# Transposes of x in one pass, the convolution accumulated in PSUM, and later modulation sums, in a hybrid Conformer and mLSTM block

## The chip, the cores and the metric

The kernel runs on one core of a Trainium2 chip. The core's engines work side by side, each in the order of its own queue: TensorE (PE, with its weight loads as PEld), VectorE (DVE), ScalarE (ACT), GpSimd (POOL), and SyncE (SP), which issues most DMA transfers. SBUF holds tiles of 128 partitions. PSUM holds eight banks of 128 x 512 fp32 numbers; TensorE writes its results there, VectorE and ScalarE read and write it. The metric is the device time of one execution in microseconds (us): 1196.62 is the median of three runs before the change (1196.0 to 1198.24).

## The reference

One layer of a backbone, all in fp32: 1024 latent tokens x of width 1024 and 256 context tokens. It computes, in order:

- Modulation: `silu(c) @ w_ada + b_ada` gives six vectors of 1024 (shift, scale and gate of the two sub-layers). The same is done for the context with `c_ctx`, of which only the first two are used here.
- `h = rms_norm(x, g0) * (1 + scale) + shift`, and the same for the context.
- One projection `h @ w_in` gives a, gl (512 each), q, k, v, o (512 each) and 16 gate columns.
- Conformer group: `u = a * sigmoid(gl)`; a depthwise convolution of width 31 along grid rows of 64 tokens; LayerNorm; silu.
- mLSTM group: four heads, two directions, chunked recurrences that begin from the context's final state; a norm per head; times `sigmoid(o)`.
- The two groups side by side through `w_out`, a norm, gate and residual; then a gated feed-forward of width 2816 with its own norm, modulation and residual.

Each output of the convolution is a sum over 31 taps:

```
y[t, c] = conv_b[c] + sum over j of conv_w[j, c] * u[t + j - 15, c]    # only within the row of 64 tokens
```

## The kernel before

Channels lie on partitions and tokens along the free dimension (xT, hT, u and accf are 128 x 1024 per block of 128 channels). Every large product is made in pieces of fp32r: operands are split into a high and a low part (`split`, `mod_apply`), and three matmuls of 512 columns (high by high, high by low, low by high) stand for one (`mm_block`, lines 150 to 154). The high part is made on ACT, the low part by a two-input subtraction on DVE or POOL (lines 134, 265 and 382).

Start (lines 397 to 452, all engines in the order written): x arrives in eight tiles of 128 tokens. For each, ACT makes the sum of squares (`x_sq`), DVE and POOL the inverse root (`rsqrt_pow`, lines 140 and 141), DVE scales the identity by it (`x_rs`, line 198), and TensorE multiplies the tile by that diagonal (`x_tr`, line 204), so that the tile comes out transposed and normalised in one fp32 product. `x_evac` copies it to xT. In between stand the load and split of the first weights and the first modulation sums (`mod_sum`, line 228: one DVE instruction over 128 x 1024 for each channel block and vector).

GLU of the first two channel blocks (j = 0, 1): for each of eight blocks k of the contraction, `mod_k` sums and scales, `mod_apply` makes h in two halves of tokens, and `glu0` issues 24 matmuls. From line 453 on a scheduler sets the order of all engines but SP; within an engine it takes what is ready by its own costs, with priorities. `glu_evac` (lines 273, 274) makes u, `conv(j)` (lines 276 to 287) the convolution: ACT writes the middle tap and the bias into accf in SBUF, and 30 DVE instructions at line 286 each add one tap in place. They have the lowest priority (`prio(100000)`), so they fill what DVE has left over while TensorE goes on with j = 2 and 3, then the v projections with the gates (`vpass`, lines 556 to 558), and the heads: the projections k, q, o with `mlstm_head` woven in. All transposes and products of a head go through `pl` or `pg` and have line 508. `conv_norm` needs all four convolutions. In PSUM two pools hold four banks each, `mm` for projections and `tp` for transposes and the heads' products. `ada_step(n)` puts the next n of 32 later modulation sums (each with its 512 KB load into one of three `raw` tiles) into the program; `proj` asks for two with each of its twelve blocks of weights.

## Time and profile before

The table is of one profiled execution, whose own time was 1197.89 us, with a span of 1195.8 us from its first instruction to its last; 2.1 us lie around the span.

| engine | busy us | share of the span | instructions |
|---|---|---|---|
| PE | 1143.2 | 96% | 5463 |
| PEld | 939.5 | 79% | 5463 |
| DVE | 932.0 | 78% | 1702 |
| ACT | 523.7 | 44% | 952 |
| POOL | 121.3 | 10% | 106 |

Shares of the whole span hide the stages. Busy time of PE is an upper figure, since its matmuls overlap and their ends are modelled. What counts for a change in one stage is what that stage's PE waits for, and which engine is full there.

### The profile page before, as it was taken

What the parts mean: (1) busy time and instruction counts of PE and PEld (TensorE: products, weight loads), DVE (VectorE), ACT (ScalarE), POOL (GpSimd) and SP (SyncE); (2) the same over time, 40 slices, a digit from 0 to 9 for tenths busy, and PEclk for the clock granted to TensorE, in tenths of its full rate; (3) what the DMA queues carried; (4) which work ended last, traced back from release to release, by engine and by line L of the source; (5) the groups of instructions that cost most, each with busy time, mean ns of one, the idle gap of its engine ahead of it and who ended that gap; (6) DMA issues with size and microseconds to landing.
All of it is one profiled execution on the core that took longest, in us unless ns stands there. A gap on an engine that the chain in (4) does not pass through costs nothing.

```text
span 1195.8 us, 14940 instructions
## 1 busy us (share of the span) xinstructions
PE 1143.2 (96%) x5463; PEld 939.5 (79%) x5463; DVE 932.0 (78%) x1702; ACT 523.7 (44%) x952; POOL 121.3 (10%) x106
## 2 busy tenths in 40 slices
PE   6899898999898999999999999999999999999997
PEld 5788787877687777887787888878888878888885
DVE  4899999999779996568966676676668685995585
ACT  6432222242485454357545344343434355454461
POOL 2634120111302210010000000000000000000000
PEclk9899899999999999999999999999999999999999
DMA  8963110442225412442324231323132159633251
GB/s 305 329 207 121 52 37 1 142 147 65 88 89 176 140 56 89 150 167 89 104 73 132 88 122 55 132 89 132 45 132 93 75 192 391 227 112 117 80 220 71
DMA packets 51823, 153.42 MB, mean 128 GB/s; under 512 B 5589, under 2 KB 5925, under 8 KB 49958
## 3 DMA queue, kind: packets, MB, share of 16 engines
q1 hardware_dynamic: 40662, 132.28, 32.0%
q10 hardware_dynamic: 11088, 20.19, 4.5%
q8 instruction: 43, 0.70, 0.2%
q14 instruction: 30, 0.25, 0.1%
HBM read 123.83 MB, written 28.61 MB: 127 GB/s over the span
## 4 chain that ended last, share of the span: by engine, by line
PE 61%; DVE 6%; ACT 1%; issue 1%; POOL 0%; DVEq 0%; POOLq 0%; ACTq 0%
PE mm L1141 8%; PE mm L1143 8%; PE mm L1142 8%; PE c L1369 3%; PE c L1371 3%; PE c L1370 3%; PE tp L1143 3%; PE tp L1142 3%; PE tp L1141 3%; PE a L1369 3%; PE a L1371 3%; PE a L1370 2%; PE mm L951 2%; PE mm L953 2%; PE mm L952 2%; PE tp L508 2%
## 5 line engine op out<-in xcount | busy, mean ns | idle before, releaser
L286 DVE SCALAR_TENSOR_TENSOR s<-t,sml,s 128x864 f32<-128x864 f32 (+14 forms) x120 | 150.5, 1295 | 0.1
L150 PE MATMUL mm<-s,w 128*128 128x512 f32 (+1 forms) x320 | 126.6, 399 | 0.0
L151 PE MATMUL mm<-s,w 128*128 128x512 f32 (+1 forms) x320 | 124.7, 393 | 0.1
L133 ACT ACTIVATE w<-raw 128x1024 fp32r<-128x1024 f32 x94 | 97.0, 1054 | 20.6 <-DMA raw<-in_w_out_dram 5.3
L1141 PE MATMUL mm<-s,w 128*128 128x512 f32 x264 | 104.9, 397 | 0.7 <-ACT h L1214 0.7
L1142 PE MATMUL mm<-s,w 128*128 128x512 f32 x264 | 104.2, 395 | 0.0
L1143 PE MATMUL mm<-s,w 128*128 128x512 f32 x264 | 104.0, 395 | 0.0
L134 DVE TENSOR_TENSOR w<-raw,w 128x1024 fp32r<-128x1024 f32 x77 | 92.3, 1222 | 1.5 <-PE mm L952 0.8
L154 PE MATMUL mm<-s,w 128*128 128x512 f32 (+1 forms) x320 | 93.2, 400 | 0.0
L141 POOL TENSOR_TENSOR r<-yw,mhalf 128x1 f32<-128x1 f32 x16 | 9.7, 608 | 690.7 <-DVE yw L140 690.7
L1141 PE MATMUL mm<-x,w 128*128 128x512 f32 x176 | 70.5, 401 | 0.7 <-ACT h L1205 0.5
L151 PEld LDWEIGHTS mm<-s,w 128*128 128x128 f32 x320 | 60.9, 190 | 11.6 <-POOL s L265 0.7
L1141 PE MATMUL tp<-s,w 128*128 128x512 f32 x176 | 69.5, 395 | 0.0
L150 PEld LDWEIGHTS mm<-s,w 128*128 128x128 f32 x320 | 61.0, 190 | 10.9
L1142 PE MATMUL tp<-s,w 128*128 128x512 f32 x176 | 69.5, 395 | 0.0
L1143 PE MATMUL tp<-s,w 128*128 128x512 f32 x176 | 69.4, 394 | 0.0
L1142 PE MATMUL mm<-x,w 128*128 128x512 f32 x176 | 69.3, 394 | 0.0
L1143 PE MATMUL mm<-x,w 128*128 128x512 f32 x176 | 69.3, 394 | 0.0
L1197 DVE TENSOR_TENSOR h<-mm,h 128x512 f32<-128x512 f32 x22 | 15.2, 692 | 66.3 <-PE mm L1143 66.3
L1271 ACT ACTIVATE s<-x 128x512 fp32r<-128x512 f32 x62 | 38.4, 628 | 64.1 <-PE a L1371 25.0
L1256 DVE TENSOR_TENSOR s<-x,s 128x512 fp32r<-128x512 f32 x62 | 42.8, 695 | 29.0 <-ACT s L1271 29.0
L154 PEld LDWEIGHTS mm<-s,w 128*128 128x128 f32 x320 | 57.0, 189 | 10.2
(311 smaller groups left out, 2916.6 us busy)
## 6 DMA issues: line engine op xcount, KB each, us to landing
raw<-in_w_up_dram SPq DMA_DIRECT2D x44, 512.0 KB, 4.5
zv<-s ACTq DMA_DIRECT2D x77, 256.0 KB, 3.4
raw<-in_w_ada_dram SPq DMA_DIRECT2D x32, 512.0 KB, 4.2
t<-in_w_ada_dram SPq DMA_DIRECT2D x28, 512.0 KB, 5.8
x<-zv SPq DMA_DIRECT2D x14, 1024.0 KB, 5.0
raw<-in_wblk_dram SPq DMA_DIRECT2D x20, 512.0 KB, 4.8
d<-in_w_down_dram SPq DMA_DIRECT2D x28, 256.0 KB, 6.8
x<-zv SPq DMA_DIRECT2D x7, 768.0 KB, 4.2
```

The costliest lines, as they stand in the source:

```text
L133: act.activation(out=hi, in_=raw, func=AF.Copy)
L134: (eng or pool).tensor_tensor(out=lo, in0=raw, in1=hi.bitcast(F32), op=ALU.subtract)
L150: pe.matmul(o, w[0][:, k], hi[:, k], start=(k == 0), stop=False)
L151: pe.matmul(o, w[0][:, k], lo[:, k], start=False, stop=False)
L154: pe.matmul(o, w[1][:, k], hi[:, k], start=False, stop=(k == KT - 1))
L286: dve.scalar_tensor_tensor(out=dst, in0=uv[:, :, lo + o:hi + o], scalar=conv_w[:, j, t:t + 1], in1=dst, op0=ALU.mult, op1=ALU.add)
L1141: pe.matmul(ps, w[0][:, s], b[0][:, k], start=(start and k == 0), stop=False, skip_group_check=True)
L1142: pe.matmul(ps, w[0][:, s], b[1][:, k], start=False, stop=False, skip_group_check=True)
L1143: pe.matmul(ps, w[1][:, s], b[0][:, k], start=False, stop=(k == 3), skip_group_check=True)
L1369: pe.matmul(ps, o[:, 0, s], o[:, 2], start=start, stop=False, skip_group_check=True)
L1370: pe.matmul(ps, o[:, 0, s], o[:, 3], start=False, stop=False, skip_group_check=True)
L1371: pe.matmul(ps, o[:, 1, s], o[:, 2], start=False, stop=stop, skip_group_check=True)
```

## The change

Five things are changed together.

- Each x tile is scaled on DVE as a whole (`x_rs` over 128 x 1024) and then transposed by TensorE against the plain identity (`pe.transpose`), in place of the product with a scaled identity. Tiles 4 to 7 are transposed by channel block (`x_trk`), in two steps of 16 transposes, each followed by its own copies.
- The start is written in another order, and the part in which all engines keep the written order now reaches to the end of the GLU of blocks 0 and 1. The row of c goes through silu before it is spread over the partitions.
- `conv(j)` accumulates in PSUM: DVE writes the middle tap and bias into a pair of banks (pool `cv`), 29 taps are added there in place, and the tap of offset 1 writes the sum to accf in SBUF; the last column of each row is copied. All four convolutions use the same pair of banks.
- For that pair, `tp` has two banks in place of four. Before the convolution the pair's halves serve as tp tiles; while it runs, one of a head's tiles comes from `mm` (`HP`); from `conv_norm` on, a pool `tp2` has the pair.
- `proj` asks for no later modulation sums with the first five blocks of weights, and for four with each of the last seven.

```diff
-    tp = wide.enter_context(tc.tile_pool(name="tp", bufs=4, space=bass.MemoryType.PSUM))
+    tp = wide.enter_context(tc.tile_pool(name="tp", bufs=2, space=bass.MemoryType.PSUM))
+    cvs = wide.enter_context(ExitStack())
+    cv = cvs.enter_context(tc.tile_pool(name="cv", bufs=1, space=bass.MemoryType.PSUM))
...
+    def CV():
+        return cv.tile([P, 2, 512], F32, tag="cv", name="cv")
...
+    def HP():
+        return MM() if conv_live == [True] else TP()
...
     def x_rs(t):
         rsqrt_pow(rst[:, t:t + 1], ss[:, t:t + 1], 1, f"x{t % 2}", 1.0 / D)
-        dgx[t] = H2(P)
-        dve.tensor_scalar(out=dgx[t], in0=ident, scalar1=rst[:, t:t + 1], scalar2=None, op0=ALU.mult)
+        dve.tensor_scalar(out=xt[t], in0=xt[t], scalar1=rst[:, t:t + 1], scalar2=None, op0=ALU.mult)
...
-                pe.matmul(ps[q][:, kk * 256 + t % 2 * P:kk * 256 + (t % 2 + 1) * P],
-                          xt[t][:, (2 * q + kk) * P:(2 * q + kk + 1) * P], dgx[t], start=True, stop=True)
+                pe.transpose(ps[q][:, kk * 256 + t % 2 * P:kk * 256 + (t % 2 + 1) * P],
+                             xt[t][:, (2 * q + kk) * P:(2 * q + kk + 1) * P], ident)
+
+    def x_trk(k0, ps):
+        for t in range(4):
+            for k in range(4):
+                pe.transpose(ps[k][:, t * P:(t + 1) * P], xt[4 + t][:, (k0 + k) * P:(k0 + k + 1) * P], ident)
+
+    def x_evack(k0, ps):
+        for k in range(4):
+            (dve.tensor_copy if k % 2 else act.copy)(out=xT[:, k0 + k, 512:1024], in_=ps[k])
...
     def conv(j):
         uv = u[j].rearrange("p (r c) -> p r c", c=W)
-        act.activation(out=accf[:, j], in_=u[j], func=AF.Identity, scale=conv_w[:, j, 15:16],
-                       bias=conv_b[:, j:j + 1])
-        for t in range(CW):
+        pair = CV().rearrange("p h n -> p (h n)")
+        pv = pair.rearrange("p (r c) -> p r c", c=W)
+        fv = accf[:, j].rearrange("p (r c) -> p r c", c=W)
+        dve.tensor_scalar(out=pair, in0=u[j], scalar1=conv_w[:, j, 15:16], scalar2=conv_b[:, j:j + 1], op0=ALU.mult,
+                          op1=ALU.add)
+        for t in (*range(15), *range(17, CW), 16):
             o = t - 15
-            if o == 0:
-                continue
             lo, hi = max(0, -o), min(W, W - o)
-            dst = accf[:, j].rearrange("p (r c) -> p r c", c=W)[:, :, lo:hi]
+            dst = (fv if o == 1 else pv)[:, :, lo:hi]
             dve.scalar_tensor_tensor(out=dst, in0=uv[:, :, lo + o:hi + o], scalar=conv_w[:, j, t:t + 1],
-                                     in1=dst, op0=ALU.mult, op1=ALU.add)
+                                     in1=pv[:, :, lo:hi], op0=ALU.mult, op1=ALU.add)
+        dve.tensor_copy(out=fv[:, :, W - 1:W], in_=pv[:, :, W - 1:W])
...
+        for t in range(4, 8):
+            x_sq(t)
+            x_rs(t)
         pA = [TP() for _ in range(4)]
-        for q in range(4):
-            x_tr(6, pA, (q,))
-            x_tr(7, pA, (q,))
-        mod_s(1)
+        x_trk(0, pA)
+        w = [split_blk(raws[2], pool)]
+        x_evack(0, pA)
+        mod_apply(0, 1)
+        mod_k(1)
+        pA = [TP() for _ in range(4)]
+        x_trk(4, pA)
...
-        ada_step(2)
+        ada_step(4 if n > 5 else 0)
...
-                pv, pc = TP(), TP()
+                pv, pc = TP(), HP()
...
     def conv_norm():
+        cvs.close()
+        conv_live[0] = wide.enter_context(tc.tile_pool(name="tp2", bufs=2, space=bass.MemoryType.PSUM,
+                                                       reuse_waits="tile"))
```

Three places show how instructions move. The first is POOL at the start, before: `rstx` is the inverse root of one x tile, `w<-raw,w` the low part of a block of weights, `s<-h,s` that of h.

```order
L141 TENSOR_TENSOR rstx<-x1w,mhalf 128x1
L141 TENSOR_TENSOR rstx<-x0w,mhalf 128x1
L265 TENSOR_TENSOR s_110<-h_254,s_108 128x512
L141 TENSOR_TENSOR rstx<-x1w,mhalf 128x1
L141 TENSOR_TENSOR rstx<-x0w,mhalf 128x1
L141 TENSOR_TENSOR rstx<-x1w,mhalf 128x1
L134 TENSOR_TENSOR w<-raw,w 128x1024
```

And POOL at the same place in the changed program:

```order
L165 TENSOR_TENSOR rstx<-x1w,mhalf 128x1
L297 TENSOR_TENSOR s_113<-h_271,s_111 128x512
L165 TENSOR_TENSOR rstx<-x0w,mhalf 128x1
L165 TENSOR_TENSOR rstx<-x1w,mhalf 128x1
L165 TENSOR_TENSOR rstx<-x0w,mhalf 128x1
L165 TENSOR_TENSOR rstx<-x1w,mhalf 128x1
L158 TENSOR_TENSOR w<-raw,w 128x1024
```

In both, the first subtraction over 128 x 1024 on POOL stands right behind the inverse root of the last x tile.

The second place is DVE in the convolution, before, around the u of block j = 3 (`t_971`); `t_725` and `t_732` are the u of blocks 0 and 1, `s_739` the accf that both add to.

```order
L286 SCALAR_TENSOR_TENSOR s_739<-t_732,sml,s_739 128x16x60
L286 SCALAR_TENSOR_TENSOR s_739<-t_725,sml,s_739 128x16x62
L286 SCALAR_TENSOR_TENSOR s_739<-t_732,sml,s_739 128x16x61
L286 SCALAR_TENSOR_TENSOR s_739<-t_725,sml,s_739 128x16x63
L286 SCALAR_TENSOR_TENSOR s_739<-t_732,sml,s_739 128x16x62
L286 SCALAR_TENSOR_TENSOR s_739<-t_725,sml,s_739 128x16x63
L286 SCALAR_TENSOR_TENSOR s_739<-t_732,sml,s_739 128x16x63
L274 TENSOR_TENSOR t_971<-mm,h_1075 128x512
```

And DVE in the changed program, in its first convolution (`t_714` is the u of block 0, `t_810` that of block 2):

```order
L320 SCALAR_TENSOR_TENSOR cv<-t_714,sml,cv 128x16x56
L320 SCALAR_TENSOR_TENSOR cv<-t_714,sml,cv 128x16x57
L320 SCALAR_TENSOR_TENSOR cv<-t_714,sml,cv 128x16x58
L320 SCALAR_TENSOR_TENSOR cv<-t_714,sml,cv 128x16x59
L320 SCALAR_TENSOR_TENSOR cv<-t_714,sml,cv 128x16x60
L320 SCALAR_TENSOR_TENSOR cv<-t_714,sml,cv 128x16x61
L320 SCALAR_TENSOR_TENSOR cv<-t_714,sml,cv 128x16x62
L320 SCALAR_TENSOR_TENSOR cv<-t_714,sml,cv 128x16x63
L306 TENSOR_TENSOR t_810<-mm,h_914 128x512
```

Two convolutions took turns before; now each tap follows the tap whose sum it reads. Of 120 taps, 2 stood right behind a tap of the same convolution before, and 63 do now.

The third place is DVE where the heads begin (`w<-tp` and `w<-w,dec,tp` are states of the context, `raw,mod<-raw,G` a later modulation sum), before:

```order
L286 SCALAR_TENSOR_TENSOR s_740<-t_971,sml,s_740 128x16x55
L228 SCALAR_TENSOR_TENSOR raw,mod<-raw,G 128x1024 x2
L286 SCALAR_TENSOR_TENSOR s_740<-t_815,sml,s_740 128x16x58
L286 SCALAR_TENSOR_TENSOR s_740<-t_971,sml,s_740 128x16x56
L286 SCALAR_TENSOR_TENSOR s_740<-t_815,sml,s_740 128x16x57
L711 COPY w<-tp 128x129
L228 SCALAR_TENSOR_TENSOR raw,mod<-raw,G 128x1024
L713 SCALAR_TENSOR_TENSOR w<-w,dec,tp 128x129
```

And now:

```order
L320 SCALAR_TENSOR_TENSOR cv<-t_810,sml,cv 128x16x56
L320 SCALAR_TENSOR_TENSOR cv<-t_810,sml,cv 128x16x55
L320 SCALAR_TENSOR_TENSOR cv<-t_810,sml,cv 128x16x54
L320 SCALAR_TENSOR_TENSOR cv<-t_810,sml,cv 128x16x53
L744 COPY w<-tp 128x129
L320 SCALAR_TENSOR_TENSOR cv<-t_810,sml,cv 128x16x52
L746 SCALAR_TENSOR_TENSOR w<-w,dec,tp 128x129
```

The sums are gone from between the first states. Up to DVE's first two-input product of a head (line 792, now 825; `t<-tp,t`), 105 taps and 11 of these sums stood in its queue before, and 104 taps and 1 sum do now. Up to the last tap there were 14 sums, and there are 8 now; from there to the end of the heads 18 before, and 24 now.

## Rows read from the trace of the kernel before

**Rows 1.** The stages: busy time of each engine in stretches of the span, in the order PE, PEld, DVE, ACT, POOL, as busy us (and instructions), then granted TensorE clock, share of the DMA engines and GB/s. The first number after the stretch is its length.

```profile
38.50:97.60 59.10, 58.99 (x256) 47.32 (x255) 56.63 (x88) 24.41 (x35) 25.36 (x16) 1.00 0.68 235
97.60:141.30 43.70, 38.73 (x199) 32.65 (x197) 43.66 (x36) 9.29 (x13) 13.42 (x9) 0.99 0.28 79
141.30:308.20 166.90, 151.08 (x913) 132.81 (x913) 165.18 (x282) 47.16 (x123) 30.45 (x14) 0.96 0.22 73
...
340.00:443.70 103.70, 98.05 (x550) 81.71 (x548) 93.30 (x354) 57.12 (x152) 17.79 (x9) 1.00 0.36 118
```

**Rows 2.** What PE waited for from 120 to 315 us: total us, times, longest us.

```profile
PE mm L556 <- DVE t L274: 5.1, 2, 3.6
PE tp L508 <- DVE h L821: 4.5, 4, 1.5
PE tp L508 <- DVE gsc L617: 3.4, 1, 3.4
PE tp L508 <- DVE ccol L601: 1.9, 1, 1.9
```

**Rows 3.** PE alone before and after its longest wait in that stretch, which ended at 141.47 us: busy us (instructions), granted clock, DMA share, GB/s.

```profile
132.00:137.00 5.00, 5.00 (x42) 1.00 0.00 0
142.00:147.00 5.00, 5.00 (x24) 0.50 0.02 5
```

**Rows 4.** DVE in order of time where the convolution begins: start us, us, what, count. Rows of one kind are merged.

```profile
97.62 8.97 DVE L286 SCALAR_TENSOR_TENSOR s<-t,sml,s 128x784 f32<-128x784 f32 x3
106.52 0.68 DVE L274 TENSOR_TENSOR t<-mm,h 128x512 f32<-128x512 f32 x1
```

**Rows 5.** POOL in order of time in the same stretch.

```profile
97.60 5.51 POOL L134 TENSOR_TENSOR w<-raw,w 128x1024 fp32r<-128x1024 f32 x2 [16.47 <-ACT w L133]
103.07 7.45 POOL L382 TENSOR_TENSOR w<-raw,w 128x816 fp32r<-128x816 f32 x3
```

**Rows 6.** Groups of DVE instructions by form, 97.6 to 112 us: count, busy us, mean ns of one, idle us before.

```profile
L286 DVE SCALAR_TENSOR_TENSOR s<-t,sml,s 128x784 f32<-128x784 f32 x2 | 5.9, 2970 | 0.0
L286 DVE SCALAR_TENSOR_TENSOR s<-t,sml,s 128x800 f32<-128x800 f32 x2 | 5.2, 2618 | 0.0
L286 DVE SCALAR_TENSOR_TENSOR s<-t,sml,s 128x816 f32<-128x816 f32 x1 | 2.2, 2155 | 0.0
```

**Rows 7.** The same view, 112 to 308.2 us.

```profile
L228 DVE SCALAR_TENSOR_TENSOR raw<-raw,G 128x1024 f32<-128x1024 f32 x14 | 16.9, 1216 | 0.1
L286 DVE SCALAR_TENSOR_TENSOR s<-t,sml,s 128x928 f32<-128x928 f32 x8 | 11.6, 1445 | 0.0
L286 DVE SCALAR_TENSOR_TENSOR s<-t,sml,s 128x912 f32<-128x912 f32 x8 | 11.4, 1429 | 0.0
L286 DVE SCALAR_TENSOR_TENSOR s<-t,sml,s 128x880 f32<-128x880 f32 x8 | 11.0, 1380 | 0.0
L286 DVE SCALAR_TENSOR_TENSOR s<-t,sml,s 128x848 f32<-128x848 f32 x8 | 10.9, 1358 | 0.0
L286 DVE SCALAR_TENSOR_TENSOR s<-t,sml,s 128x1008 f32<-128x1008 f32 x8 | 10.0, 1260 | 0.0
...
L286 DVE SCALAR_TENSOR_TENSOR s<-t,sml,s 128x800 f32<-128x800 f32 x6 | 7.8, 1315 | 0.0
...
L286 DVE SCALAR_TENSOR_TENSOR s<-t,sml,s 128x784 f32<-128x784 f32 x6 | 6.2, 1034 | 0.0
...
L713 DVE SCALAR_TENSOR_TENSOR w<-w,dec,tp 128x129 f32<-128x129 f32 x16 | 4.9, 339 | 0.0
```

**Rows 8.** DVE in order of time: four taps in which two convolutions take turns, then two taps of one convolution in a row.

```profile
136.03 4.78 DVE L286 SCALAR_TENSOR_TENSOR s<-t,sml,s 128x1008 f32<-128x1008 f32 x4
...
267.20 2.54 DVE L286 SCALAR_TENSOR_TENSOR s<-t,sml,s 128x992 f32<-128x992 f32 x2
```

**Rows 9.** The middle tap on ACT, all four convolutions.

```profile
L278 ACT ACTIVATE s<-t,sml 128x1024 f32<-128x1024 f32 x4 | 5.0, 1243 | 37.6 <-DVE t L274 37.6
```

**Rows 10.** DVE in order of time: the scaling of a 128 x 1024 tile in SBUF by a column, once beside a POOL instruction and once alone.

```profile
144.42 2.87 DVE L347 TENSOR_SCALAR t<-t,rsc 128x1024 f32<-128x1024 f32 x1 [0.60 <-POOL rsc L141]
...
147.29 0.74 DVE L347 TENSOR_SCALAR t<-t,rsc 128x1024 f32<-128x1024 f32 x1
```

**Rows 11.** The start, in order of time: DVE and POOL around the last x tile, then PE and DVE where PE's stream begins.

```profile
30.49 2.35 DVE L198 TENSOR_SCALAR h<-ident,rstx 128x128 f32<-128x128 f32 x1 [0.66 <-POOL rstx L141]
...
29.91 0.55 POOL L141 TENSOR_TENSOR rstx<-x1w,mhalf 128x1 f32<-128x1 f32 x1 [2.81 <-DVE x1w L140]
30.43 2.34 POOL L134 TENSOR_TENSOR w<-raw,w 128x1024 fp32r<-128x1024 f32 x1
...
32.90 5.87 PE L204 MATMUL tp<-h,t 128*128 128x128 f32 x28 [4.69 <-DVE h L198]
38.84 0.39 PE L151 MATMUL tp<-s,w 128*128 128x512 f32 x1
39.07 0.39 PE L154 MATMUL tp<-s,w 128*128 128x512 f32 x1
...
39.42 1.22 DVE L228 SCALAR_TENSOR_TENSOR t<-t,G 128x1024 f32<-128x1024 f32 x1
```

**Rows 12.** What PE waited for from 308.2 to 450 us.

```profile
PE tp L508 <- DVE h L821: 3.1, 3, 1.7
PE tp L508 <- DVE dn L818: 1.7, 1, 1.7
```

More of the change, by code (lines that the diff above doesn't have):

```diff
@@ L83, in MM @@
         return mm.tile([P, 512], F32, tag="mm", name="mm")
-    def TP():
+    def CV():
+        return cv.tile([P, 2, 512], F32, tag="cv", name="cv")
+    conv_live = []
+    halves_left = []
+    tp_turn = [0]
+    def TP():
+        if conv_live != [True]:
+            tp_turn[0] += 1
+            if conv_live and tp_turn[0] % 2:
+                return conv_live[0].tile([P, 512], F32, tag="tp2", name="tp")
+            if not conv_live and tp_turn[0] % 4 in (3, 0):
+                if not halves_left:
+                    pair = CV()
+                    halves_left.extend((pair[:, 1], pair[:, 0]))
+                return halves_left.pop()
         return tp.tile([P, 512], F32, tag="tp", name="tp")
+    def HP():
+        return MM() if conv_live == [True] else TP()
     def H2(n=512):
@@ L472, in hybrid_block @@
             glu0(1, k)
-        nxt_w = load_pair(2)
+            if k == 5:
+                nxt_w = [split_blk(raws[0], pool)]
+    nxt_w.append(split_blk(raws[1], pool))
     ada_step(16)
@@ L480, in hybrid_block @@
     accf = wide_tile(4, 2)
+    for j in (0, 2):
+        dve.memset(accf[:, j, 0:1], 0.0)
+    conv_live.append(True)
     vw = None
```

81 lines of the change are left out of this document (33 added, 48 removed).

## Prediction

> **What bounds the kernel now.** I read the busy times by stretch first, then PE's waits in the stretches where it is not full, then DVE and POOL in order of time around those waits, last DVE's groups by form. From 38.5 to 97.6 us PE works 58.99 of 59.10 us, but DVE is just as full (56.63); from 97.6 to 308.2 us DVE is busy for 43.66 of 43.70 and 165.18 of 166.90 us while PE has gaps [rows 1]. Almost all that PE waits for there are results that DVE gives late: a PSUM bank that `glu_evac` has yet to read, the gates, the heads [rows 2]. So from 97.6 to 308.2 us DVE's queue sets the pace. [...] From 340 us on PE is the fuller engine, though DVE is busy for 93.30 of 103.70 us until 443.7 [rows 1].
>
> Part of DVE's fullness is not work. While POOL makes its subtractions from 97.6 to 110.5 us [rows 5], a tap of 784 elements takes 2.97 us; later, with POOL idle, the same form takes 1.03 [rows 6, 7]. In that very stretch, at 106.52, `glu_evac` takes 0.68 us [rows 4]: of its two inputs one is in PSUM. So a DVE instruction with both inputs in SBUF is held up by POOL, and one with an input in PSUM is not.
>
> **The change part by part**, against the profiled execution's 1197.9 us, which is 1.3 over the median of the runs shown.
>
> *Taps in PSUM, freed of POOL.* Each tap now reads u from SBUF and its sum from PSUM, as line 713 reads w and `tp`. Held-up taps of the first group cost 5.9 + 5.2 + 2.2 us for five; undisturbed, at 1.03 us for 784 and 1.01 ns more per element (from 1034 at 784 and 1260 at 1008 [rows 7]), they cost 5.2: 8.1 gained. In the later group the forms 928, 912, 880, 848 and 800 stand above that line by 8 x 0.27 + 8 x 0.27 + 8 x 0.25 + 8 x 0.26 + 6 x 0.26 = 10 us, one blocked tap in each. Together **-18.1 us** of DVE.
>
> *The price of a tap in PSUM.* That reading costs nothing extra shows at line 713: 0.339 us for 129 columns, where the taps' line gives 0.37 [rows 7]. No row has DVE write PSUM. From below I bound it by those 0.03 us (120 taps: -4 us); from above the furthest row is a tap that takes 2.97 where 1.03 would do (+1.94, or 233 us in all). I take 0, since line 713 is the same operation with the inputs placed as now. [...]
>
> *Taps in a chain.* Four taps in which two convolutions take turns span 4.78 us, though they take 3 x 1.26 + 1.24 = 5.02 one by one: each begins 0.08 before the last ends. Two of one convolution in a row, of 992 and 1008 elements, take 2.54: their own 1.24 (by the line) + 1.26 and 0.035 of a gap [rows 7, 8]. A tap right behind its predecessor thus costs 0.115 more. There were 2 such pairs and are now 63 (order of the change): 61 x 0.115 = **+7.0 us**. [...]
>
> *Middle taps.* ACT made them in 1.24 us each [rows 9]; DVE makes them now at 1.28 (the taps' line at 1024), and copies a last column of 16: 4 x 1.28 + 4 x 0.15 = **+5.7 us**. That ACT is freed gains nothing: it was not waited for.
>
> *Later sums.* Six of 1.22 us [rows 7] leave the stretch before the last tap: **-7.3 us**. At the start of the first head ten have left, so DVE is ahead there by 5 us more, and the waits for gates and states shrink most.
>
> *Start.* 64 transposes in one pass save PE time that it spends waiting anyway: the last scaling held it for 4.69 us, because POOL's subtraction began at 30.43, right behind its inverse root, and held DVE's scaling, which began at 30.49, until its end [rows 11]. The new order puts the same subtraction in the same place (order of POOL), and the scaling is now one of 128 x 1024 within SBUF, which takes 0.74 alone and 2.87 beside POOL [rows 10]. Tiles 4 to 7 follow each other on DVE and POOL with some 1.45 us each (a column, 0.55, 0.74, two handovers) from about 22 us; POOL's subtraction starts near 27 and the last scaling ends near 30. Behind it stand 16 transposes, their copies, 16 more (which need the banks of the first), `mod_apply`, and the low part of the fourth block of weights. I get PE's unbroken stream near 41 us with 24 matmuls done, against 38.5 with 6 [rows 11]; at 0.23 us a matmul before has 17 done by 41, so PE leads by 1.6 us. But DVE is full from here on, and its sums of k = 2 begin near 40.2, behind that low part, in place of 39.42 [rows 11]: **+0.8 us**. Loads keep ahead, since tiles wait for DVE, not for SP. Bounds -3 and +3.
>
> *Half the tp banks.* An update of a state now waits for the second one before it, not the fourth. They come in pairs 8 matmuls (1.85 us) apart, and DVE needs two of 0.34 and one tap of 1.1 for a pair: just covered. I take 0; uncovered, each of 16 updates [rows 7] could cost one tap, 17 us.
>
> *Sum to the last tap.* -18.1 + 7.0 + 5.7 - 7.3 + 0.8 = **-11.9 us**. PE can follow: its waits on rows 2 alone are 17 us, and the slow clock behind them comes on top. PE's queue also has some ten more matmuls ahead of the last transposes of `conv_norm`: -2.
>
> *After the last tap.* The six sums come back here, 7.3 us for a DVE that has 10.4 us idle from 340 to 443.7 [rows 1]. An ordered queue cannot always use its holes, and PE waits for DVE there already [rows 12]. Bounds 0 and 7.3; I take +3, nearer to what the holes can hide. Behind 443.7 us nothing changes.
>
> Forecast: 1197.9 - 11.9 - 2 + 3 = **1187 us**.
>
> **Rivals.** *More is won*: the chain costs nothing, or the two convolutions' order matters less, and the late sums hide. For it: ten of the sums leave just where PE waits most, and each avoided long wait also spares the slow clock [rows 3]. Against: rows 8. 1187 - 7 - 3 = 1177.
>
> *The gain is handed back late*: with 24 sums in DVE's queue behind the last tap and four loads into three `raw` tiles ahead of each block of weights, PE waits for heads or weights. For it: DVE's 93.30 of 103.70 us. Against: until now no weights were waited for there [rows 12]. All 7.3 and as much again in late weights, less the 3 counted: 1187 + 9 = 1196 to 1202.
>
> *Slower: DVE reads and writes one PSUM bank in the same instruction, and pays for it.* Its place is the 120 taps. It decides from (11.9 + 2 - 3) / 120 = 0.09 us a tap; were the streaming part to double (on average 896 columns at 1.01 ns, 0.9 us), the time would be 1187 + 108 = 1295. For it: no row shows such a write. Against: line 713 for the reading half.
>
> **How the numbers follow.** Forecast 0.45 (own range 1181 to 1193), more won 0.25, handed back late 0.15, slower 0.15. What a measurement here can tell from no change is 0.2%, 2.4 us. Faster: the first two, and a fifth of the third at its lower edge, less a little of the forecast's: 0.72. Slower: all of the fourth and a third of the third: 0.20. Same: the rest, 0.08. The range goes from 1173, under the second case, to 1201, over most of the third and the mild part of the fourth; some 0.05 lies below and 0.13 above.
>
> **What would show it.** Right: taps in PSUM on the old line (1.03 us at 784, 1.26 at 1008) whatever POOL does, 0.035 between them; PE's waits for line 274 and the gates gone, with no stretch at half clock between 138 and 148; the last tap near 296 us; DVE fuller and PE's waits longer between 330 and 430. Wrong: taps above 1.1 us at 784, PE waiting for weights, or a start in which the GLU's stream begins after 43 us, which would push everything behind it.

## The result, and the profile after the change

The kernel got slower: 1215.67 us (median, 1211.87 to 1219.29) against 1197.43 in the same batch, a ratio of 1.015 with a 95% interval of 1.0123 to 1.0176. The profiled execution took 1215.12 us, with a span of 1213.4. The forecast was 1187 us.

The busy time of each engine by stretch, first of the kernel before and then of the changed one. The edges are the first tap, the first statistics of `conv_norm` (called A below) and the last product with `w_out` (B). Columns: length, busy time of each engine, PE's granted clock, share and rate of DMA.

```profile
0.00:97.60 97.60, 84.89 (x391) 69.45 (x392) 75.25 (x130) 47.77 (x71) 36.80 (x40) 0.97 0.75 270
97.60:309.20 211.60, 190.53 (x1118) 166.16 (x1116) 209.85 (x323) 56.44 (x136) 43.87 (x23) 0.97 0.23 74
309.20:536.40 227.20, 219.87 (x1140) 180.27 (x1139) 169.54 (x555) 120.71 (x275) 33.69 (x34) 1.00 0.38 125
536.40:1195.80 659.40, 647.95 (x2819) 523.57 (x2817) 477.39 (x697) 298.82 (x471) 6.95 (x11) 1.00 0.35 126
```

```profile
0.00:103.90 103.90, 85.04 (x332) 63.18 (x333) 85.17 (x131) 51.09 (x75) 45.99 (x43) 0.90 0.74 264
103.90:311.80 207.90, 190.74 (x1138) 168.34 (x1137) 194.49 (x324) 51.82 (x131) 27.66 (x20) 0.97 0.18 57
311.80:554.90 243.10, 223.68 (x1116) 182.73 (x1115) 174.26 (x558) 123.10 (x276) 33.40 (x34) 0.96 0.39 129
554.90:1213.40 658.50, 647.10 (x2819) 524.03 (x2817) 477.31 (x697) 298.94 (x471) 6.91 (x11) 1.00 0.36 126
```

Read the third busy column, DVE. In the second stretch its work fell by 15.4 us (209.85 to 194.49); the prediction's terms for it (-18.1, +7.0, +5.7, -7.3) come to -12.7. But the stretch is only 3.7 us shorter: DVE idles for 13.4 us where it idled for 1.75. The stretch behind it grew by 15.9 us, with only 4.7 us more work of DVE. And the first tap comes 6.3 us later, behind 9.9 us more of DVE's work (75.25 to 85.17), so that up to A this work fell by 5.4 us in all. So 6.3 - 3.7 + 15.9 - 0.9 makes the 17.6 us of span.

Why the first tap is late, ACT, POOL and DVE show in order of time (start, duration, instruction), first of the kernel before:

```profile
95.33 1.24 ACT L278 ACTIVATE s<-t,sml 128x1024 f32<-128x1024 f32 x1 [6.71 <-DVE t L274]
96.48 1.05 ACT L133 ACTIVATE w<-raw 128x1024 fp32r<-128x1024 f32 x1
```

```profile
87.82 1.06 ACT L157 ACTIVATE w<-raw 128x1024 fp32r<-128x1024 f32 x1 [0.59 <-DMA raw<-in_wblk_dram]
88.96 5.80 POOL L158 TENSOR_TENSOR w<-raw,w 128x1024 fp32r<-128x1024 f32 x2 [4.33 <-ACT w L157]
89.08 3.42 DVE L260 SCALAR_TENSOR_TENSOR t<-t,t 128x1024 f32<-128x1024 f32 x1
92.44 2.35 DVE L266 TENSOR_TENSOR AB<-mod,b 128x8 f32<-128x8 f32 x1
95.85 1.90 DVE L267 TENSOR_TENSOR AB<-AB,sml 128x8 f32<-128x8 f32 x1
```

Before, ACT waited 6.71 us for u to make a middle tap, the high part of the next weights stood behind that in its queue, and POOL's subtraction of their low part began at 97.60 [rows 5], together with the taps. With the middle taps on DVE, ACT makes that high part 8.7 us earlier, and POOL's subtractions fall on what DVE does ahead of the last `glu_evac` and the first tap: a sum for the context and two operations over 128 x 8, which take 1.2 and twice 0.2 us undisturbed, and 7.7 here. So POOL still holds DVE up, for 6.1 us, only not in the taps; and the first middle tap, 1.35 us, now stands ahead of the first tap on DVE. All runs agree: where the middle taps are on ACT the first tap comes at 95.7 to 97.6 us, where they are on DVE at 102.8 to 105.1, also with the old start (e3) and with the taps in SBUF and four `tp` banks (e6).

The taps themselves, grouped by form (instructions, busy us and mean ns, idle time before them), answer to [rows 7]:

```profile
L320 DVE SCALAR_TENSOR_TENSOR cv<-t,sml,cv 128x784 f32<-128x784 f32 x8 | 8.3, 1036 | 0.2
L320 DVE SCALAR_TENSOR_TENSOR cv<-t,sml,cv 128x1008 f32<-128x1008 f32 x4 | 5.1, 1272 | 0.1
L313 DVE TENSOR_SCALAR cv<-t,sml 128x1024 f32<-128x1024 f32 x3 | 4.0, 1347 | 0.1
```

1036 ns at 784 and 1272 at 1008, for 1034 and 1260 before, beside POOL or not: the longest of all 120 takes 1273. Reading and writing PSUM cost the taps next to nothing (2 to 12 ns each), and POOL no longer holds a tap up.

What PE waits for between the first tap and A answers to [rows 2] (total us, times, longest):

```profile
PE tp L388 <- DVE h L393: 7.4, 1, 7.4
PE mm L174 <- DVE h L854: 4.0, 1, 4.0
PE mm L589 <- DVE t L306: 2.0, 1, 2.0
PE mm L589 <- DVE h L598: 1.5, 1, 1.5
```

The old waits have shrunk (L306 is the old line 274: 2.0 us, for 5.1). Two new ones lead. L388 are the context's 16 transposes in `ctx_prepare`: they fill four tp tiles, and with two banks the second half, PE's next work at 154 us, must wait for copies (L393) that stand behind eight taps in DVE's queue:

```profile
150.68 3.44 DVE L320 SCALAR_TENSOR_TENSOR cv<-t,sml,cv 128x848 f32<-128x848 f32 x3
154.16 2.37 DVE L320 SCALAR_TENSOR_TENSOR cv<-t,sml,cv 128x896 f32<-128x896 f32 x2
156.56 3.69 DVE L320 SCALAR_TENSOR_TENSOR cv<-t,sml,cv 128x928 f32<-128x928 f32 x3
160.24 1.89 DVE L393 TENSOR_SCALAR h<-tp,AB 128x256 f32<-128x256 f32 x4
```

Until 275.8 us a projection (L174) waits for an mm bank that a head took by `HP()`. Around the first of the two waits PE does this (same columns as the stretches above):

```profile
153.00:161.30 8.30, 0.98 (x8) 0.77 (x7) 8.19 (x12) 0.04 (x1) 0.00 (x0) 0.84 0.00 0
161.30:170.00 8.70, 8.63 (x55) 8.66 (x56) 6.57 (x14) 3.14 (x8) 0.00 (x0) 0.76 0.01 2
```

8 matmuls in 8.3 us, and then a granted clock of 0.76 in the records: PE pays twice, as it did at [rows 3], where the clock was 0.50.

Behind A, DVE's sums and, up to the last head at 474 us, its waits, of the changed kernel, and the sums of the kernel before:

```profile
L260 DVE SCALAR_TENSOR_TENSOR raw<-raw,G 128x1024 f32<-128x1024 f32 x24 | 29.2, 1218 | 7.1 <-DMA raw<-in_w_ada_dram 7.0
```

```profile
DVE raw L260 <- DMA raw<-in_w_ada_dram: 7.0, 5, 1.9
```

```profile
L228 DVE SCALAR_TENSOR_TENSOR raw<-raw,G 128x1024 f32<-128x1024 f32 x18 | 21.8, 1211 | 0.0
```

24 sums in place of 18, and before five of them DVE stands for 7.0 us in all because their loads have not landed. PE's waits there, up to 480 us:

```profile
PE tp L541 <- DVE h L854: 7.6, 5, 2.3
PE tp L541 <- DVE h L865: 4.8, 2, 3.7
PE tp L541 <- DVE dn L849: 1.7, 1, 1.7
```

L854 is the old line 821, which had 3.1 us of waits before [rows 12]. L849 is the old line 816, two steps ahead of the L818 for which PE waited 1.7 us then.

At the start the transposes of x are 64 records of PE (L225, L232) where the products were 128 (L204), one every 0.11 us at full clock in both. The GLU's stream begins as forecast: at 41 us 20 of its matmuls have begun (17 before), at 76 us 168 (166 before). Then it starves: 177 against 192 at 82 us, 247 against 269 at 100. DVE in order of time shows why (start, duration, instruction):

```profile
68.32 2.32 DVE L260 SCALAR_TENSOR_TENSOR t<-t,t 128x1024 f32<-128x1024 f32 x1
...
71.63 1.22 DVE L260 SCALAR_TENSOR_TENSOR t<-t,G 128x1024 f32<-128x1024 f32 x1
...
73.99 1.22 DVE L260 SCALAR_TENSOR_TENSOR t<-t,t 128x1024 f32<-128x1024 f32 x1
...
75.20 0.16 DVE L268 TENSOR_TENSOR AB<-mod,sml 128x1 f32<-128x1 f32 x1
```

And in the kernel before:

```profile
70.44 0.16 DVE L235 TENSOR_TENSOR AB<-AB,sml 128x1 f32<-128x1 f32 x1
...
73.97 1.47 DVE L228 SCALAR_TENSOR_TENSOR t<-t,t 128x1024 f32<-128x1024 f32 x1 [1.53 <-ACT t L310]
```

`t<-t,G` is the first of the two sums that the last block of the GLU needs (the second follows at 72.77), `t<-t,t` are sums for the context, which nothing waits for yet. The scheduler put four of these (from 61.27 us on; three are stretched to 2.3 us by POOL) ahead of the last block's scale. That is ready at 75.4 us; before, all the context's sums came behind it, and it was ready at 70.6.

### The profile page after: what moved, and what is told of

Its sections match the earlier page's. It is cut to its first block, busy times and chain, and to the rows that moved or that the text cites. A ratio compares the mean times of both kernels' runs of the same rounds, so it can differ in the third digit from the quotient of the medians.

```text
span 1213.4 us, 14790 instructions
## 1 busy us (share of the span) xinstructions
PE 1146.6 (94%) x5399; PEld 938.3 (77%) x5399; DVE 931.2 (77%) x1710; ACT 524.9 (43%) x952; POOL 114.0 (9%) x106
## 4 chain that ended last, share of the span: by engine, by line
PE 72%; DVE 20%; ACT 3%; issue 3%; DMA 2%; POOL 1%; SPq 0%; DVEq 0%; POOLq 0%; ACTq 0%
PE mm L1177 8%; PE mm L1178 8%; PE mm L1179 8%; DVE cv L320 4%; PE tp L541 4%; PE tp L1177 3%; PE tp L1179 3%; PE tp L1178 3%; PE c L1405 3%; PE c L1407 3%; PE c L1406 3%; DVE t L260 3%; PE mm L174 3%; PE mm L175 3%; PE a L1405 2%
## 5 line engine op out<-in xcount | busy, mean ns | idle before, releaser
L174 PE MATMUL mm<-s,w 128*128 128x512 f32 (+1 forms) x320 | 131.0, 413 | 11.5 <-ACT s L296 5.5
L320 DVE SCALAR_TENSOR_TENSOR cv<-t,sml,cv 128x784 f32<-128x784 f32 (+14 forms) x116 | 133.2, 1148 | 2.2
L175 PE MATMUL mm<-s,w 128*128 128x512 f32 (+1 forms) x320 | 129.1, 407 | 3.9 <-POOL s L297 3.9
L178 PE MATMUL mm<-s,w 128*128 128x512 f32 (+1 forms) x320 | 91.5, 401 | 0.0
L174 PEld LDWEIGHTS mm<-s,w 128*128 128x128 f32 x320 | 62.8, 196 | 24.4 <-ACT s L296 6.6
L175 PEld LDWEIGHTS mm<-s,w 128*128 128x128 f32 x320 | 62.7, 196 | 17.5 <-POOL s L297 5.8
L178 PEld LDWEIGHTS mm<-s,w 128*128 128x128 f32 x320 | 57.8, 191 | 10.6
```

The source lines that it names most:

```text
L174: pe.matmul(o, w[0][:, k], hi[:, k], start=(k == 0), stop=False)
L175: pe.matmul(o, w[0][:, k], lo[:, k], start=False, stop=False)
L178: pe.matmul(o, w[1][:, k], hi[:, k], start=False, stop=(k == KT - 1))
L320: dve.scalar_tensor_tensor(out=dst, in0=uv[:, :, lo + o:hi + o], scalar=conv_w[:, j, t:t + 1], in1=pv[:, :, lo:hi], op0=ALU.mult, op1=ALU.add)
```

## The experiments

Each ran together with the kernel before, whose medians are 1196.55 to 1197.49 us. A and B are as above: where `conv_norm` begins, and the length from there to the last product with `w_out`. "PE" is PE's busy time in that second part, so that the rest of its length are PE's gaps; "sums" are the later sums of full size in it.

| run | us | ratio (95%) | A | A to B | PE | sums |
|---|---|---|---|---|---|---|
| before | 1197 | | 309.2 | 227.2 | 219.9 | 18 |
| after | 1215.7 | 1.015 (1.0123 to 1.0176) | 311.8 | 243.1 | 223.7 | 24 |
| e1 after, sums as before | 1217.1 | 1.0165 (1.0151 to 1.0179) | 323.3 | 234.7 | 218.7 | 18 |
| e2 before, sums late | 1204.7 | 1.0065 (1.0052 to 1.0077) | 303.5 | 241.6 | 229.9 | 25 |
| e3 before, convolution in PSUM | 1214.5 | 1.0148 (1.0132 to 1.0163) | 319.8 | 233.9 | 213.5 | 18 |
| e4 before, new start | 1202.8 | 1.0046 (1.0034 to 1.0059) | 308.8 | 233.1 | 226.8 | 18 |
| e5 before, banks alone | 1211.2 | 1.0121 (1.0107 to 1.0135) | 315.5 | 234.9 | 226.9 | 18 |
| e7 e3, context in halves | 1209.7 | 1.0115 (1.0096 to 1.0133) | 314.0 | 234.0 | 213.8 | 18 |
| e8 before, low parts on DVE | 1202.7 | 1.0040 (1.0028 to 1.0053) | 304.0 | 238.1 | 219.1 | 18 |
| e9 before, sums early | 1215.4 | 1.0151 (1.0137 to 1.0165) | 330.3 | 225.2 | 211.5 | 8 |
| e10 e8, sums early | 1205.1 | 1.0064 (1.0050 to 1.0078) | 320.3 | 225.0 | 210.6 | 8 |
| e11 e7, sums early | 1217.0 | 1.0158 (1.0141 to 1.0176) | 331.9 | 223.9 | 212.0 | 8 |
| e12 after, context in halves | 1212.6 | 1.0132 (1.0118 to 1.0146) | 308.7 | 242.8 | 223.6 | 24 |
| e13 after, sums cut short | 1191.5 | 0.9947 (0.9935 to 0.9960) | 297.2 | 233.7 | 226.9 | 4 |
| e18 after, context's copies on ACT | 1205.8 | 1.0077 (1.0063 to 1.0090) | 306.1 | 238.3 | 225.6 | 24 |

A is not the moment at which the taps end. In e2, e13 and e18 the last tap ends at 280.3, 290.4 and 299.0 us, and `conv_norm` begins 23.2, 6.8 and 7.1 us later, when PE comes to it. How far PE has come by then shows in what it has left: 219.9 us before, 213.5 in e3, 229.9 in e2. So A and the length behind it are read together with this column.

### The parts alone

The first theory, from the trace alone, blamed the late sums. e1 gives the changed kernel its old sums back, e2 gives the late sums to the kernel before; e3 and e4 are the other two parts alone: the pools, `HP()`, `conv` and `conv_norm` of the change's diff, and its `x_rs`, `x_tr`, `x_trk` and the new order of the start.

```diff
-        ada_step(4 if n > 5 else 0)
+        ada_step(2)
```

(e1; e2 is the same line the other way round, in the kernel before.)

> The changed kernel with two later sums in each of the twelve blocks of weights, as before the change. Theory LATE (the sums that were moved behind the last tap fill DVE where the heads alone set the end, and their loads come late): the stretch from the last tap to the first product with w_out, 152 us after the change, goes back to about 136, and six sums (7.3 us) return to the convolution's stretch, where DVE had 11 us idle: 1198 to 1205 us. Rival START (the loss comes from the start and the two banks, and the sums hide): no gain, 1213 to 1218, since the convolution's stretch gets longer by what the end gets shorter.

> The kernel before with the later sums moved alone. LATE: the last tap is earlier by 5 to 7 us (six sums fewer ahead of it), the stretch behind it longer by 10 to 17: 1200 to 1210 us. Rival START: the sums use DVE's idle time behind the last tap, so 1190 to 1197.

> The kernel before with the convolution in PSUM and its pools alone (old start, two sums a block). If the two banks that are gone cost nothing, DVE does 5 to 6 us less by the last tap, and PE's waits there shrink: 1188 to 1193 us. Rival BANKS (with two tp banks and one mm bank for a head, PE and DVE wait for each other, as at 161 and 276 us after the change): the gain is eaten, 1196 to 1204, with a wait of over 4 us for the context's transposes and one for an mm bank.

> The kernel before with the new start alone (one-pass transposes, fixed order to the end of the first GLU). The first tap comes 6 us later as after the change. Since DVE is full from there to the last tap, START says that all 6 arrive at the end: 1202 to 1205 us. Rival: PE and DVE make up for it (PE was ahead, DVE's waits shrink): 1196 to 1199.

e1: 1217.1, no gain. LATE falls for the changed kernel, though its half is there: A to B became 8.4 us shorter (243.1 to 234.7), and A came 11.5 us later. e2: 1204.7, as LATE had said, with A earlier by 5.7 and A to B longer by 14.4, though 10.0 of these are work that PE has left, and the last tap came 27.9 us earlier, not 5 to 7. So what six or seven sums cost behind A they cost ahead of it too, and moving them is worth +7.8 us or nothing, by what else is in the kernel. e3 is the finding: the convolution in PSUM, which was to bring most of the gain, costs 17.7 us by itself, nearly all that the whole change loses. e4: the new start costs 6.0, as START had said, but not in its way: the first tap comes at 95.8 us, 1.9 earlier than before, and A 0.4 earlier. The loss arrives behind A, where PE has 6.9 us more to do. The three parts (e2, e3, e4) add up to 31.5 us, the whole to 18.2; they are not independent.

### Banks or taps

What of e3 comes from the two tp banks that it takes? e5 has the pools and `HP()` of the change, but the old convolution in SBUF. e6 has the old pools, and in SBUF one convolution at a time in the changed order. e7 is e3, with the second half of `ctx_prepare` two token blocks later.

The edit of e5 in the kernel before, with `CV()`, `TP()` and `HP()` as in the change:

```diff
-    tp = wide.enter_context(tc.tile_pool(name="tp", bufs=4, space=bass.MemoryType.PSUM))
+    tp = wide.enter_context(tc.tile_pool(name="tp", bufs=2, space=bass.MemoryType.PSUM))
+    cvs = wide.enter_context(ExitStack())
+    cv = cvs.enter_context(tc.tile_pool(name="cv", bufs=1, space=bass.MemoryType.PSUM))
...
-                pv, pc = TP(), TP()
+                pv, pc = TP(), HP()
```

That of e6, whose next convolution takes its bias from a column that the last one writes:

```diff
-        act.activation(out=accf[:, j], in_=u[j], func=AF.Identity, scale=conv_w[:, j, 15:16],
-                       bias=conv_b[:, j:j + 1])
-        for t in range(CW):
+        bias = cbt[:, j:j + 1] if j else conv_b[:, 0:1]
+        dve.tensor_scalar(out=accf[:, j], in0=u[j], scalar1=conv_w[:, j, 15:16], scalar2=bias, op0=ALU.mult,
+                          op1=ALU.add)
+        for t in (*range(15), *range(17, CW), 16):
...
+        if j < 3:
+            dve.scalar_tensor_tensor(out=cbt[:, j + 1:j + 2], in0=accf[:, j, 0:1], scalar=0.0,
+                                     in1=conv_b[:, j + 1:j + 2], op0=ALU.mult, op1=ALU.add)
```

And that of e7:

```diff
+            if k2 == 2:
+                yield
...
             if pas and i == 5:
-                ctx_prepare()
+                cg = ctx_prepare()
+                next(cg)
+            if pas and i == 7:
+                run(cg)
```

> The kernel before with two tp banks in place of four and one mm bank for a head (the pair for the convolution is there but the taps stay in SBUF, two convolutions interleaved as before). Theory BANKS (the 17.7 us of the convolution in PSUM come from the banks that it takes: the context's transposes wait for their copies, and the heads for tp and mm banks): 1205 to 1215 us, with the wait of about 7 us in front of the context's transposes. Rival TAPS (they come from the taps in a chain, one convolution at a time, with which DVE cannot fill its holes): 1195 to 1201 us.

> The kernel before, four tp banks, taps in SBUF, but with the middle tap on DVE, the changed order of taps, and each convolution begun only when the one before it is done (a column of 0.06 us ties them). TAPS: DVE has 7 us of handovers and 5 us of middle taps more and nothing to fill its holes with: 1207 to 1215 us. BANKS: the last tap is late by some 12 us, but PE is not held up: 1196 to 1203.

> The convolution in PSUM alone (1214.5 us) with the context's 16 transposes in two halves, the second half two blocks of tokens later in the program, so that two tp banks do for each half. BANKS: the wait of 7.2 us at 156 us and the slow clock behind it go: 1205 to 1209 us. TAPS: that wait only moves PE's idle time, since the last tap and the products behind it come no earlier: 1212 to 1216.

e5 is BANKS: 14.2 us slower with not one tap changed. PE's waits in it, from the first tap to A:

```profile
PE tp L377 <- DVE h L382: 7.5, 1, 7.5
PE tp L533 <- DVE gsc L642: 4.8, 1, 4.8
PE mm L581 <- DVE t L298: 4.3, 2, 3.6
PE mm L174 <- DVE h L846: 3.8, 1, 3.8
PE tp L533 <- DVE w L736: 3.6, 1, 3.6
```

The first is the context's transposes again, the fourth the mm bank; the second and third were there before; the fifth is the update of a state, which waits here for 3.6 us. Up to A this kernel loses 6.3 us, and behind it 7.7, where PE has 7.0 us more left to do. e7 gains 4.9 us on e3, just short of what BANKS had expected. There the first wait, 7.2 us in e3, is halved, not gone: 3.5 us in two, the longest 3.2.

e6 took 1224.6 us (1.0228), but cannot be read for TAPS, since one wait is nearly as long as its loss of 27.6 us:

```profile
PE mm L562 <- DVE s L367: 25.4, 1, 25.4
```

In this program's order the context's low part came late in DVE's queue, and `vpass` stood for it. It shows how long a queue full of taps can keep PE from a short instruction; a price of the chain it does not give. That is read from the changed kernel's own records: 60 pairs of taps one behind the other, each 35 ns apart, 2.1 us.

The same question was put to the changed kernel: e12 has the halves of e7, e18 leaves the order and moves the eight scalings that empty the banks to ACT, whose queue holds no taps.

```diff
-                dve.tensor_scalar(out=tmp[:, kk * 256:(kk + 1) * 256], in0=ps[:, kk * 256:(kk + 1) * 256],
-                                  scalar1=AB[:, 1, k:k + 1], scalar2=AB[:, 3, k:k + 1], op0=ALU.mult, op1=ALU.add)
+                act.activation(out=tmp[:, kk * 256:(kk + 1) * 256], in_=ps[:, kk * 256:(kk + 1) * 256],
+                               func=AF.Identity, scale=AB[:, 1, k:k + 1], bias=AB[:, 3, k:k + 1])
```

> The changed kernel with the context's transposes in two halves, as its only edit. BANKS: the wait of 7.4 us at 161 us and some 3 us of slow clock go, and stay gone: 1205 to 1209 us. TAIL: PE is ahead after 200 us and waits for the heads behind the last tap, so most of it is handed back: 1211 to 1216 us.

> The changed kernel, with the same eight scalings on ScalarE, whose queue holds no taps. If the wait of 7.4 us at 161 us is one for DVE's queue, it goes with two banks too: 1208 to 1212 us, as with the transposes in halves (1212.6). If two banks are too few whoever empties them, it stays at over 4 us: 1214 to 1217.

(TAIL in the first of these is the theory formed on e8, below.) e12: 1212.6, some 3 us; there too the wait only shrank, to 3.5 us, so it tells little between the two. e18: 1205.8, 9.9 us less than the changed kernel (medians of two batches, with before at 1197.43 and 1196.55), and below both expectations. PE's waits in e18 from the first tap to A begin so:

```profile
PE mm L174 <- DVE h L854: 5.1, 2, 3.6
PE tp L541 <- DVE gsc L650: 3.7, 1, 3.7
PE mm L589 <- DVE h L598: 1.5, 1, 1.5
```

No wait for the context's transposes is left, with two banks. So it was no wait for a bank as such, but one for DVE's queue, which two banks let PE feel and four did not. That the edit takes 4 us of work from DVE is not what gains: in the kernel before, with four banks, the same edit brings nothing (e17, below). The wait can explain the part ahead of A, 5.7 us; another 4.8 come behind A, which the edit does not touch, and have no shown cause.

### Where the sums and DVE's work lie

e8 frees the taps from POOL in another way: the low parts that POOL made before the last tap are made on DVE. e9 to e11 put the later sums early.

```diff
-            ahead[order[n]] = load_blk(order[n])
-        ada_step(2)
+            ahead[order[n]] = load_blk(order[n], dve if n < 6 else None)
+        ada_step(4 if n < 7 else 0)
```

(e8 has the first of the two lines, e9 the second, e10 both; e8 and e10 also make the low parts of block 8 and in `v_split` on DVE.)

> The kernel before with the low parts of the weights of the value projections and of the first six blocks of the heads' projections made on DVE and not on POOL, so that POOL holds up no tap: each subtraction costs DVE 1.22 us and saves the 1.9 us that it made a tap longer, so 0.7 x 8 to 14 = 6 to 10 us of DVE. If DVE's amount of work before the last tap sets the time, 1187 to 1192 us; if it does not (the later sums moved alone brought the last tap from 307 to 279 us and the end no earlier), 1194 to 1199.

> The kernel before with four later sums in each of the first six blocks of weights and none in the last six, the opposite of the change. Theory TAIL (what comes behind the last tap is bound by DVE's share of the heads; PE that is ahead there has only used up the products that cover the heads): some twelve sums (15 us of DVE) leave the heads' stretch and delay the taps by as much, 1190 to 1196 us. Rival FRONT (DVE's work before the last tap sets the end): 1203 to 1213 us.

> The kernel before with the weights' low parts on DVE before the last tap (1202.7 us) and the later sums early. TAIL: the DVE time freed before the last tap is used by the sums, and the heads' stretch gets shorter: 1186 to 1194 us. FRONT: 1204 to 1214 us.

> The convolution in PSUM alone, the context's transposes in two halves (1209.7 us), and the later sums early. TAIL: 1196 to 1204 us. FRONT: 1212 to 1222 us.

e8: 1202.7, slower, against both expectations, and yet `conv_norm` begins 5.2 us earlier. A to B is 10.9 us longer: PE is ahead at A and, so the reading that became TAIL, has fewer products left to cover the heads with. Here are the two stretches of e8, as in the first fences:

```profile
96.80:304.00 207.20, 198.69 (x1183) 173.66 (x1182) 203.24 (x342) 57.34 (x137) 13.64 (x12) 0.99 0.23 76
304.00:542.10 238.10, 219.09 (x1076) 178.42 (x1075) 170.45 (x546) 120.67 (x274) 33.05 (x34) 0.94 0.36 120
```

PE worked 198.69 of 207.20 us in the first, and then lost 19 us to gaps, with a clock of 0.94, in the second. The second holds 546 DVE instructions (555 before) and is longer all the same.

TAIL, formed on that, falls as a rule for the end: e9 to e11 take 18, 8 and 20 us more than the kernel before, and e10 and e11 also 2.4 and 7.4 more than e8 and e7, from which they come. With 8 sums behind A the length from there is 224 to 225 us, with 18 it is 227 to 238, with 24 or 25 it is 238 to 243. But that does not show that the sums make the length: in e9 to e11 PE has only 211 to 212 us left, and gaps of 12 to 14 us in place of 7.3, and e13, with four sums of full size, has 233.7. FRONT is right about the rest: ten sums more ahead of A, 12 us of DVE, make it 21 us later (e9).

Does DVE's time for a sum do this, or its load? In e13 the 28 sums of the last seven blocks take 8 of their 1024 columns, and all loads stay.

```diff
-                mod_sum(r, s, w, ch, k)
+                if cut[0]:
+                    mod_sum(r[:, 0:8], s[:, 0:8], w, ch, k)
+                else:
+                    mod_sum(r, s, w, ch, k)
```

> The changed kernel; the 28 later sums of the last seven blocks of weights take only 8 of their 1024 columns (the rest of each sum is left out), all their loads stay. Theory DVE (the stretch from conv_norm to the last mixing product lasts as long as DVE's work in it, sums included): the stretch falls from 243 us to about 225 or less, the time to 1193 to 1199 us. Rival LOADS (the sums hold DVE up because their loads come late, and the loads cost by themselves): DVE still waits for them, 1207 to 1213.

(`cut[0]` holds for the last seven blocks.) 1191.5 us, 24 less than the changed kernel, for 28 x (1.22 - 0.16) = 30 us of DVE: DVE's time. The length from A to B, though, fell to 233.7, not to the 225 expected. The sums still wait for their loads there, and that costs little:

```profile
L260 DVE SCALAR_TENSOR_TENSOR raw<-raw,G 128x8 f32<-128x8 f32 x20 | 3.0, 159 | 5.7 <-DMA raw<-in_w_ada_dram 5.7
```

Of the 24 us, 14.6 show up before A, though only 8 of the 28 sums lay there.

Three edits then took work from DVE in the kernel before, and none gained: e14 (the heads' normalisation, on ACT; e16 is e8 with it), e15 (later sums of the last seven blocks) and e17 (the edit of e18).

```diff
+        nb = SM(4, "hnb")
+        dve.scalar_tensor_tensor(out=nb, in0=mv[:, 4 * g:4 * g + 4, 0], scalar=-1.0, in1=rs, op0=ALU.mult, op1=ALU.mult)
         for t in range(4):
-            dve.tensor_scalar(out=hh[:, t], in0=hh[:, t], scalar1=mv[:, 4 * g + t, 0:1], scalar2=rs[:, t:t + 1],
-                              op0=ALU.subtract, op1=ALU.mult)
+            act.activation(out=hh[:, t], in_=hh[:, t], func=AF.Identity, scale=rs[:, t:t + 1], bias=nb[:, t:t + 1])
```

```diff
-                mod_sum(r, s, w, ch, k)
+                if cut[0]:
+                    for q in range(4):
+                        c = slice(q * 256, (q + 1) * 256)
+                        pool.tensor_tensor(out=r[:, c], in0=r[:, c], in1=s[:, c], op=ALU.mult)
+                    act.activation(out=r, in_=r, func=AF.Copy, accum_out=mod[:, w, ch, k:k + 1])
+                else:
+                    mod_sum(r, s, w, ch, k)
```

> The kernel before; the normalisation in head_tail (32 scalings of 128x128, 0.34 us each) goes from DVE to ACT, with one small DVE product for each group of four in its place. DVE: some 26 of them lie in the stretch behind conv_norm, 7 us of DVE less, of which the tight places count: 1191 to 1195 us. Rival ORDER (the heads' chain of handovers, not DVE's amount, sets that stretch; ACT's handover is longer): 1196 to 1202.

> The kernel before; the later sums of the last seven blocks of weights are made by GpSimd (product, in four pieces) and ScalarE (sum), not by DVE. DVE: 14 sums, 17 us of DVE, leave the stretch behind conv_norm, whose length falls from 227 towards 218: 1188 to 1194 us. Rival LOCK (GpSimd's two-input products hold up DVE's small two-input operations of the heads, as they did the taps): 1198 to 1210.

> The low parts of the weights on DVE before the last tap (1202.7 us) and the normalisation in head_tail on ACT. DVE: the lead that PE has before conv_norm (18 us less lost than before) is kept in part, since DVE has 7 us less behind it: 1193 to 1198 us. ORDER: 1201 to 1206.

> The kernel before, with the context's eight scalings out of PSUM (0.54 us each, 3.7 us of DVE in a row) on ScalarE. If DVE's amount of work before the last tap is what counts, 1192 to 1196 us. If the order that comes of it counts for more (as with the normalisation of the heads on ScalarE, which gained nothing), 1197 to 1203.

e14: 1200.2 (1.0029, 1.0019 to 1.0039); e16: 1200.9 (1.0030, 1.0020 to 1.0040); e17: 1197.8 (1.0010, 1.0001 to 1.0019); e15: 1213.4 (1.0132, 1.0118 to 1.0146). The kernel before shows how much longer ACT's handover, of which ORDER speaks, is: where ACT waited for DVE, it began 0.093 us after DVE's end (median of 134 waits), and where DVE waited for ACT, 0.033 us after ACT's (64 waits). For e15 the trace shows LOCK in part: two-input operations of the heads were held up by POOL even at 128x2.

```profile
L825 DVE TENSOR_TENSOR dn<-dn,thr x20: 128/154/2347, 359.0 to 447.9; 128x2 f32<-128x2 f32 x20
```

The median is 154 ns, the longest 2347. But that longest one, at 379.33 us, runs beside a subtraction of weights, which the kernel before has as well (2353 ns there). Beside the new products the holds are short:

```profile
374.64 2.81 POOL L302 TENSOR_TENSOR raw<-raw,G 128x256 f32<-128x256 f32 x4
376.70 0.76 DVE L824 SCALAR_TENSOR_TENSOR dn<-dn 128x2 f32<-128x2 f32 x1
379.29 2.37 POOL L134 TENSOR_TENSOR w<-raw,w 128x1024 fp32r<-128x1024 f32 x1 [1.84 <-ACT w L133]
```

Over all of them, measured against the median of the same instruction, they take some 12 us from DVE, of the 17 that the 14 sums had. The rest of e15's loss has no shown cause. The others say that a few us of DVE less are not enough. In e14 DVE's work behind A fell by 5.6 us (169.54 to 163.94) and the length from A to B grew by 3.6; in e17 DVE's idle time before A went from 1.75 to 4.4 us. Every edit makes the scheduler order DVE and PE anew, so what a single edit moves by less than some 5 us is not put down to its mechanism here; that holds for the gains of e7 and e12 too. No run beat the kernel before except e13, which leaves work out.

## Why the prediction was wrong

**Right.** *Taps in PSUM* and their price of 0: 1036 ns at 784 and 1272 at 1008. Counted from the end of the instruction before each, the 120 taps take 134.0 us of DVE in place of 146.1, and 2.1 of gaps: 10.0 us gained where -18.1 + 7.0 = -11.1 were forecast. So the rival of a bank read and written at once fell. *Middle taps*, as work of DVE: 4 x 1.35 + 4 x 0.18 = 6.1 us, for 5.7. *Later sums*: six left the stretch before A (14 to 8), as counted. PE's waits for the old line 274 and the gates shrank, and the granted clock from 138 to 153 us is 1.00. The GLU's stream began near 41 us. Two of the sums do not come out as written: the lines of [rows 2] make 14.9 us, not 17, and 7.3 + 7.3 - 3 in the second rival is 11.6, not 9. Neither moves the outcome.

**Wrong first, and for most: "Half the tp banks ... I take 0".** The forecast looked only at the updates of the states, and these were indeed nearly covered: the updates (L746) are not among PE's waits before A. It did not list who else takes tp tiles four at a time. `ctx_prepare` does, and its copies stand in DVE's queue behind taps: 7.4 us of waiting and a slow clock behind it (0.76 from 161.3 to 170 us). Taking it away is worth 9.9 us (e18), where the same edit with four banks is worth nothing (e17). `HP()` moved another wait of 4.0 us to the projections' banks. The banks alone cost 14.2 us (e5). The 17 us that the forecast named as a bound, for the updates, has that size by luck; its range, up to 1201, was not widened for it.

**Wrong second: "Sum to the last tap", which took each term for itself and the last tap for the end of the stretch.** DVE's work behind the first tap did fall by 15.4 us, but the stretch by 3.7. Most of the difference is the first mistake again: with the banks alone (e5) the stretch is 7.3 us longer, for 1.5 us less of DVE's work. Where only sums were cut short (e13, against the changed kernel), 10.7 us less of DVE made it 14.8 us shorter. The rest lies ahead of the first tap. "That ACT is freed gains nothing" left out what stood behind the middle taps in ACT's queue: POOL's subtractions now begin ahead of the taps and cost DVE 6.1 us there, so little is left of the 8.1 us of which the first taps were freed. e3 differs from e5 by the convolution alone: that costs 3.5 us (17.7 for 14.2), where -18.1 + 7.0 + 5.7 = -5.4 was forecast. The last tap, forecast near 296, ended at 309.9; in e2 it ended 27.9 us earlier than before, and `conv_norm` began only 5.7 earlier.

**Wrong third: "After the last tap ... I take +3", of bounds 0 and 7.3.** 15.9 us. The six sums come to 7.3 us, and the waits for their loads are 7.0; that the two add up is not shown, since in e13 the waits stay at 5.7 us and cost little. PE's work left there grew by 3.8 us, its gaps by 12.1. This is the rival of the gain handed back late, with its mechanism half right: late were the loads of the sums, not those of weights. Yet undoing it does not help (e1), since the same sums cost 11.5 us ahead of A. No place was found in this kernel where DVE has room for them: e13 is worth 24 us. The forecast's 10.4 us of idle time did not take up the sums.

**Wrong fourth: "Start +0.8", bounds -3 and +3.** 6.0 us alone (e4). The loss is not where it was looked for, but at the last block of the GLU, to which DVE came late because of four sums for the context. By 100 us PE has 22 matmuls of 0.23 us less done, 5.1 us; in e4 it is 16, 3.7 us. There it is not made up, and shows only behind A, in the 6.9 us more that PE has left.

What stays open: how the 14.2 us of the banks divide among the context's transposes, the mm bank and the updates; how much of the 13 us by which the single parts together cost more than the whole is the scheduler's order; why e14's 5.6 us less of DVE bring nothing while e13's 30 bring 24; and what e18 gains behind A. A price for taps in a chain beyond the 35 ns was not found, since e6 broke elsewhere.

## What to carry to other kernels

When a change takes banks or buffers, list every place that fills several of them at once, and look in whose queue the instruction stands that frees them: a short instruction behind a row of long fillers cost PE 7.4 us in one wait here, and 25.4 in e6. When an instruction leaves an idle engine's queue, list what stood behind it: that starts earlier (here 8.7 us), and what it feeds may now fall on an engine that is full (here for 6.1 us). What work saved on a full engine is worth depends on what else is changed with it: here 30 us less of DVE brought 24, and 5 to 7 us less brought nothing (e8, e14, e17); price such a term at a part, and keep the whole loss in the range. Low-priority work that is moved out of a full stretch must be priced where it arrives.
